# Four edits to the order of high and low weight products and to the PSUM banks of the output mix in a one-core decoder layer

## The chip, the cores and the metric

The kernel runs as one program on one core of a Trainium2 chip. The metric is device time in microseconds, the median of several runs. A core has a matrix engine (TensorE, PE in the rows; its weight loads are PEld), a vector engine (DVE), a scalar engine (ACT), GpSimd (POOL), and a queue engine (SP) that issues most transfers. Each engine runs its own instructions in the order in which the program wrote them and waits for the others by semaphores. Products accumulate in PSUM, of which the program uses eight banks of 128 x 512 fp32 numbers, in two pools of four.

## The reference, cut to what matters

A decoder layer for 256 tokens of width 1024, in fp32, with 256 memory tokens:

```python
z = h @ w_in[l]                      # u (512), q, k, v (512 each)
pool_out = multiscale_pool(u, w_pool[l], pool_scale[l])
attn_out = moba_attention(q, k, v).reshape(B_, S_, ATTN_WIDTH)
mix = jnp.concatenate([pool_out, attn_out], axis=-1) @ w_out[l]
h = layer_norm(DEEPNORM_ALPHA * h + mix, ln1_g[l], ln1_b[l])
h = layer_norm(DEEPNORM_ALPHA * h + memory_cross_attention(h, mem, w_xq[l], w_xkv[l], w_xo[l]), ...)
h = layer_norm(DEEPNORM_ALPHA * h + swiglu(h, w_gate[l], w_up[l], w_down[l]), ...)
```

`u` are the pooling inputs, the first half of `mem @ w_xkv` are the memory keys, `mix` is the output projection of the first block, and the gate and up products of `swiglu` are 11 chunks of 256 + 256 columns.

## The kernel before

**Precision.** Every operand of a product is split in a rounded high part and a remainder, the low part (suffixes h and l in the names): ACT makes the high part (a cast), DVE the low part (a subtraction). A product is high by high, high by low and low by high. `proj_both` takes the token side as one 512-wide moving operand (high and low next to each other), so that a high weight needs one 512-wide matmul (L431) and a low weight one 256-wide matmul (L437).

**Blocks.** The weights of one column chunk come as tiles of several k rows. `proj_both(pss, numbers, yT, group)` does the high matmuls of `group` k rows, two or four matmuls for each, and then the low ones of the same k rows. With group = 8 (KD) all highs of a chunk stand in a row, then all lows. Before the change the pooling inputs (`do_u`, tiles w15 to w18, 2 chunks of two tiles) and the memory keys (`do_xk`, w19 to w26, 4 chunks) use 4, which is one tile of highs, one of lows; the gate and up chunks use 8, the last three of them (w91 to w102) 2, which is one tile as well.

**Weights.** `Stream` fetches raw tiles on SP (7 raw buffers) and prepares them (L184 cast on ACT, L191 subtraction on DVE) into 8 buffers, 9 late in the kernel. It prepares one tile more when a matmul asks for a high row (`get`; every third or second asking in the stages of u and xk) and when a tile is done with (`done`, `next`). So the place of a preparation in the ACT and DVE queues follows from the order in which the matmuls are written.

**Order around the change.** The stages are generators that are run a few steps at a time, with other work written between: `run(u, 4)`, `probs_t(0)`, `run(u, 6)`, `scores(1, 0)` and so on. `scores` puts q k products in two banks (ps), DVE takes them with the maximum (L605), ACT the exponential (L574). `attend` writes po. `split_mem(0)` and `split_mem(4)` split the memory tokens into mT, k rows 0 to 3 and 4 to 7, on ACT (L483) and DVE (L484): the rows print both halves as mT, the order tells them apart as mT_88 and mT_89. The keys of memory use mT: w19, the first tile of a chunk, the first half, w20, the second tile, the second half. `pool_diff` (L657) and `mix_pool` (pm, L661) finish the pooling.

**Banks.** Two pools of four banks each are dealt round robin: `accbank` for the long sums (pu, pxk, acc, xv, m), `bank` for the short ones (ps, pt, po, pm, tp). A tile waits for the last reader of the tile that had its bank before. `project` does the mix (c_mix, w27 to w34) into four accumulators, one for each PIECE (token tile t by column half), first for all four k row by k row, and at the end piece by piece, so that the norm can begin (L768). The last chunk of memory keys holds two accbanks until DVE has taken them (L691, L693).

Of the kernel before, what the change touches and what calls it, by code (L numbers as in the profile page):

```python
# [18 lines left out]
KD = D // P  # L19
# [5 lines left out]
NFC = DFF // CW  # L25
# [25 lines left out]
class Stream:  # L51
# [148 lines left out]
    def get(self, numbers, k):  # L200

        n = self.src[numbers[0]].shape[1]
        self.prepare(numbers[k // n] + 1)
        self.asked += 1
        if not self.held and self.asked % self.pace == 0:
            self.prepare(min(self.used + self.ahead, len(self.tiles) + 1))
        return self.parts_of(numbers, k)
# [18 lines left out]
def decoder_layer(  # L226
# [15 lines left out]
    def a8(name, dt=F32):  # L242
        return ap.tile([P, KD, S], dt, tag="a8", name=name)

    def bank(name):
        return pb.tile([P, 512], F32, tag="b", name=name)

    def accbank(name):
        return pa.tile([P, 512], F32, tag="acc", name=name)
# [4 lines left out]
    def cols(w, c):  # L254

        return ws.add(w[c])

    def rows(w, k0, c0, nk=1, width=D):
        return ws.add(w[k0 * P:(k0 + nk) * P, c0:c0 + width].rearrange("(k p) n -> p k n", p=P), 1)
# [16 lines left out]
    c_u = [cols(w_u, c) for c in range(2)]  # L276
    c_xk = [cols(w_xk, c) for c in range(4)]
    c_mix = [rows(w_out, k, 0) for k in range(KD)]
# [4 lines left out]
    c_xo = [rows(w_xo, k, 0) for k in range(KD)]  # L283
    c_gu = [ws.add(w_gu[c], 4) for c in range(NFC)]
# [38 lines left out]
    xT, mT = Both("xT"), Both("mT")  # L323
# [5 lines left out]
    home = [ap.tile([P, 4, 512], F32, tag="a8", name=f"wr{i}") for i in range(2)]  # L329
# [93 lines left out]
    def proj_both(pss, numbers, yT, group=KD):  # L423

        for k0 in range(0, KD, group):
            for k in range(k0, k0 + group):
                hi, _ = ws.get(numbers, k)
                for b, ps in enumerate(pss):  # L430
                    nc.tensor.matmul(ps, hi[:, b * P:(b + 1) * P], yT.both(k), start=k == 0, stop=False,  # L431
                                     skip_group_check=True)
                yield
            for k in range(k0, k0 + group):
                _, lo = ws.parts_of(numbers, k)
                for b, ps in enumerate(pss):
                    nc.tensor.matmul(ps[:, S:], lo[:, b * P:(b + 1) * P], yT.pair(k)[0], start=False,  # L437
                                     stop=k == KD - 1, skip_group_check=True)
                ws.done(numbers, k)
                if ws.pace == 1:  # L440
                    ws.next()
                yield
# [10 lines left out]
    def proj_rows(acc, chunks, get, pieces, first, last, free, again=False):  # L453

        last_k = sum(ws.rows(numbers) for numbers in chunks) - 1
        k0 = 0
        for numbers in chunks:
            nk = ws.rows(numbers)
            for t in sorted({piece[0] for piece in pieces}):
                for j in range(nk):  # L460
                    k = k0 + j
                    y = pair(get(k), ALL, slice(t * P, (t + 1) * P))
                    hi, lo = ws.get(numbers, j)
                    for piece in pieces:
                        if piece[0] == t:
                            s = slice(*piece[1:])
                            three(acc[piece], y, (hi[:, s], lo[:, s]), first and k == 0, last and k == last_k,
                                  again)
                    if free and t == pieces[-1][0]:
                        ws.done(numbers, j)  # L470
                    yield
            k0 += nk
# [139 lines left out]
    cT = (a8("cTh", F32R), a8("cTl", F32R))  # L612
# [31 lines left out]
    def windows(c):  # L644

        cur, n = upad[:, 2 * c:2 * c + 2, :], 1
        for j, g in enumerate((2 * c, 2 * c + 1)):
            while n < WINDOWS[g]:
                nxt = ep.tile([P, 2, PADW + S], F32, name="win", bufs=4)
                nc.gpsimd.tensor_add(nxt[:, j:, 2 * n - 1:], cur[:, j:, 2 * n - 1:], cur[:, j:, n - 1:PADW + S - n])  # L650
                cur, n = nxt, 2 * n
            sums[g] = cur[:, j, :]
            nc.gpsimd.tensor_mul(sums[g][:, PADW:2 * PADW], sums[g][:, PADW:2 * PADW], fac[:, g, :])
# [20 lines left out]
    def do_u():  # L674
        for c in range(2):
            pss = [accbank("pu") for _ in range(2)]
            yield from proj_both(pss, c_u[c], xT, 4)
            for f, ps in enumerate(pss):
                y = upad[:, 2 * c + f, PADW:]
                nc.scalar.copy(y, ps[:, S:])  # L680
                nc.vector.tensor_add(y, ps[:, :S], y)  # L681
            windows(c)
# [3 lines left out]
    def split_both(hi, lo, left, pss):  # L686

        for f, ps in enumerate(pss):
            nc.scalar.copy(hi[:, f], ps[:, :S])  # L689
        for f, ps in enumerate(pss):  # L690
            nc.vector.tensor_sub(left[:, f], ps[:, :S], r32(hi[:, f]))  # L691
        for f, ps in enumerate(pss):
            nc.vector.tensor_add(lo[:, f], ps[:, S:], left[:, f])  # L693

    def do_xk():
        for c in range(4):
            pss = [accbank("pxk") for _ in range(2)]
            yield from proj_both(pss, c_xk[c], mT, 4)
            left = sp.tile([P, 2, S], F32, name="xkl", tag="pr", bufs=PR_BUFS)
            split_both(*[y[:, 2 * c:2 * c + 2, :] for y in xkT], left, pss)  # L700

# [50 lines left out]
    class Norm:  # L752
# [13 lines left out]
        def sum(self, c0, c1, acc):  # L766
            s = slice(c0, c1)
            nc.vector.scalar_tensor_tensor(self.r[:, s], self.tok[:, s], ALPHA, acc, op0=OP.mult, op1=OP.add)  # L768
# [36 lines left out]
    HALVES = ((0, 512), (512, D))  # L805
    PIECES = tuple((t, *half) for t in range(T) for half in HALVES)

    def project(chunks, get, held, pieces=PIECES):

        acc = {piece: accbank("acc") for piece in PIECES}
        if pieces != PIECES:
            (*_, (_, _, c), _), last = pieces, PIECES[-1]
            acc[pieces[-2]], acc[pieces[-1]] = acc[last][:, :c - last[1]], bank("acc")[:, :last[2] - c]
        head, rest = chunks[:-held], chunks[-held:]
        done = sum(ws.rows(numbers) for numbers in head)
        if head:
            yield from proj_rows(acc, head, get, PIECES, True, pieces != PIECES, True)
        ws.prepare(ws.used + ws.ahead)  # L820
        ws.prepare(ws.used + ws.ahead, nc.gpsimd)
        ws.held = True
        for piece in pieces:
            yield from proj_rows(acc, rest, lambda k: get(done + k), [piece], not head or piece[1] % 512 != 0, True,
                                 piece == pieces[-1], bool(head) and pieces != PIECES)
            yield piece, acc[last] if pieces != PIECES and piece == pieces[-2] else acc[piece]
# [8 lines left out]
    load_norm("g", 1, ln1_g)()  # L835
    load_norm("b", 1, ln1_b)()
    h1 = ap.tile([P, T, D], F32, tag="a8", name="h1")
    mix = project(c_mix, lambda k: (cT[0][:, k], cT[1][:, k]), 4)
    for t in range(T):
        norm = Norm(1, t, xt[:, t, :], h1[:, t, :])  # L840
        for half in HALVES:
# [24 lines left out]
    oT = (a8("oTh", F32R), a8("oTl", F32R))  # L866
# [37 lines left out]
    def xattend(h):  # L904
        po = bank("xo").rearrange("p (d t) -> p d t", d=2)
        for dd in range(2):
            for s in range(2):
                c = h * 256 + dd * P
                three(po[:, dd, :], pair(xv, ALL, s, slice(c, c + P)), pair(xpt[h], ALL, s), s == 0, s == 1)
        split(oT[0][:, 2 * h:2 * h + 2, :], oT[1][:, 2 * h:2 * h + 2, :], po)  # L910
# [17 lines left out]

    h2T = Both("h2T")
    h2 = ap.tile([P, T, D], F32, tag="a8", name="h2")  # L930
    xo = project(c_xo, lambda k: (oT[0][:, k], oT[1][:, k]), 4)
    xattend(1)
    run(xo, 1)
    xprobs_t(2)
# [116 lines left out]
    for c in range(1, NFC):  # L1051
        pss = [(accbank if c % 2 else bank)("pg") for _ in range(4)]
        if c == 3:
            ws.widen(late)
            for i in range(2):
                add_quarters(i)
        gu = proj_both(pss, c_gu[c], h2T, KD if c < NFC - 3 else 2)
        run(gu, 2)
        if left:
            left.multiply()  # L1060
        run(gu, 2)
        if left:
            left.split()
        else:
            run(gu, 4)
            gated_t()
        if c == NFC - 1:
            run(gu, 7)
            ws.held = True
        run(gu)  # L1070
        left = Gated(c, pss)
        left.add()
# [128 lines left out]
    acc = until(dn)  # L1201
# [71 lines left out]
```

## Time and profile before

| | |
|---|---|
| median of 3 runs | 376.22 us (376.06 to 376.52) |
| span of the profiled execution, first to last instruction | 374.4 us |
| left outside the span, median less span | 1.8 us |
| PE busy | 367.9 us, 98% of the span |
| DVE busy | 301.2 us, 80% |
| ACT busy | 206.2 us, 55% |
| chain that ended last | PE 97% |

No time of the profiled execution is given beside its span. A busy PE is a modelled one: a matmul's record is longer than the step to the next, so short waits of PE show as a longer step between two starts rather than as idle time. Times in rows are microseconds from the span's start.

### The profile page before, as it was taken

The numbers are of one execution on the slowest core, as the hardware profiler recorded it, in microseconds if no ns is written. First come the engines' busy times: TensorE is split into PE (matmuls) and PEld (weight loads), VectorE is DVE, ScalarE is ACT, GpSimd is POOL, SyncE is SP. The second block draws the span as 40 slices with busy tenths as digits, with TensorE's granted clock in tenths as the row PEclk, the third lists the DMA queues.
The fourth block names the chain that finished last, engine by engine and source line by source line (L and its number), as shares of the span: only waits on it lengthen the run. The fifth ranks groups of instructions, "written<-read, shape, count | busy, mean of one in ns | idle before, by whom it ended". The sixth has DMA issues, their size and how long they took to land.

```text
span 374.4 us, 5619 instructions
## 1 busy us (share of the span) xinstructions
PE 367.9 (98%) x2058; PEld 317.1 (85%) x2058; DVE 301.2 (80%) x487; ACT 206.2 (55%) x330; POOL 23.6 (6%) x31
## 2 busy tenths in 40 slices
PE   9999999999999999999999999999999999999994
PEld 8997878787888889998888988888888888888882
DVE  6768899975599677875899478888888996999994
ACT  6656677644154645644237456766655575774610
POOL 1000033400020000000112000000000000000012
PEclk9999999999999999999999999999999999999998
DMA  8997684568508964588439999955557463896302
GB/s 279 415 415 268 210 293 136 204 210 285 183 0 271 396 203 141 191 297 306 164 61 293 282 302 335 351 179 175 193 192 251 151 188 98 275 354 258 112 2 112
DMA packets 25819, 84.51 MB, mean 226 GB/s; under 512 B 2624, under 2 KB 3392, under 8 KB 25664
## 3 DMA queue, kind: packets, MB, share of 16 engines
q1 hardware_dynamic: 24528, 78.98, 60.3%
q0 software_dynamic: 832, 4.72, 6.3%
q10 hardware_dynamic: 432, 0.46, 0.4%
q8 instruction: 16, 0.26, 0.3%
q14 instruction: 11, 0.09, 0.1%
HBM read 83.10 MB, written 10.49 MB: 250 GB/s over the span
## 4 chain that ended last, share of the span: by engine, by line
PE 97%; DMA 1%; DVE 1%; ACT 0%; issue 0%; POOLq 0%; ACTq 0%
PE pg L431 20%; PE pg L437 10%; PE pqk L537 6%; PE m L417 5%; PE m L418 5%; PE m L416 5%; PE acc L416 4%; PE acc L417 4%; PE acc L418 4%; PE pxk L431 4%; PE pxq L431 4%; PE pxq L437 2%; PE pu L431 2%; PE pxk L437 2%; PE xv L416 2%; PE xv L418 2%
## 5 line engine op out<-in xcount | busy, mean ns | idle before, releaser
L483 ACT CAST g<-sg 128x512 fp32r<-128x512 f32 x16 | 9.9, 620 | 21.0 <-DVE sg L1037 15.1
L779 POOL TENSOR_TENSOR rs<-rs,mhalf 128x1 f32<-128x1 f32 x6 | 5.0, 833 | 257.6 <-DVE rs L778 257.6
L484 DVE TENSOR_TENSOR g<-sg,g 128x512 fp32r<-128x512 f32 x16 | 11.1, 692 | 9.6 <-ACT g L483 9.6
L1018 DVE TENSOR_TENSOR sg<-pg,sg 128x256 f32<-128x256 f32 x40 | 14.1, 415 | 2.7 <-ACT sg L1017 2.7
L1017 ACT COPY sg<-pg 128x256 f32<-128x256 f32 x40 | 11.8, 376 | 3.8 <-PE pg L437 3.8
L1022 ACT ACTIVATE sg<-sg 128x512 f32<-128x512 f32 x10 | 6.4, 635 | 11.2 <-DVE sg L1018 11.2
L574 ACT ACTIVATE xpr<-xs,mx 128x256 f32<-128x256 f32 x8 | 3.7, 470 | 14.3 <-DVE mx L585 14.3
L574 ACT ACTIVATE pr<-pr,mx 128x128 f32<-128x128 f32 (+1 forms) x16 | 7.1, 445 | 7.6 <-DVE mx L605 7.6
L483 ACT CAST h2T<-tp 128x512 fp32r<-128x512 f32 x4 | 2.3, 587 | 13.0 <-PE tp L494 12.9
L784 DVE SCALAR_TENSOR_TENSOR r<-r,mv,gb 128x512 f32<-128x512 f32 (+2 forms) x12 | 8.2, 722 | 0.0
L771 DVE BATCH_NORM_STATS2 st<-r 128x6 f32<-128x512 f32 (+1 forms) x12 | 8.0, 671 | 0.3
L650 POOL TENSOR_TENSOR win<-upad 128x542 f32<-128x542 f32 x2 | 4.0, 2000 | 57.0 <-DVE upad L681 57.0
L1023 DVE TENSOR_TENSOR sg<-sg 128x512 f32<-128x512 f32 x10 | 6.9, 691 | 0.8
L579 DVE RECIPROCAL sm<-sm 128x2 f32<-128x2 f32 x12 | 2.0, 166 | 6.0 <-ACT xpr L574 4.5
L889 PE MATMUL xs<-xkTh,xq 128*128 128x256 f32 x32 | 6.4, 282 | 0.0
L483 ACT CAST h1T<-tp 128x512 fp32r<-128x512 f32 x4 | 2.4, 588 | 7.2 <-PE tp L494 7.2
L789 DVE SCALAR_TENSOR_TENSOR h<-r,rs,gb 128x512 f32<-128x512 f32 x8 | 5.7, 747 | 0.1
L650 POOL TENSOR_TENSOR win<-win 128x269 f32<-128x269 f32 (+3 forms) x4 | 5.8, 1446 | 0.2
L689 ACT CAST xkTh<-pxk 128x256 fp32r<-128x256 f32 x8 | 2.6, 377 | 5.5 <-PE pxk L437 5.5
L691 DVE TENSOR_TENSOR xkl<-pxk,xkTh 128x256 f32<-128x256 f32 x8 | 3.0, 416 | 3.1 <-ACT xkTh L689 3.1
L889 PEld LDWEIGHTS xs<-xkTh,xq 128*128 128x128 f32 x32 | 5.2, 190 | 0.2
L184 ACT CAST w39h<-w39r 128x1024 fp32r<-128x1024 f32 x1 | 1.0, 1049 | 7.8 <-PE acc L418 7.8
(1137 smaller groups left out, 1289.6 us busy)
## 6 DMA issues: line engine op xcount, KB each, us to landing
sum_z<-in_w_sum SPq DMA_DIRECT2D x2, 1536.0 KB, 9.4
sum_z<-in_w_sum POOLq DMA_DIRECT2D x2, 1536.0 KB, 15.4
gb<-in_ln_g SPq DMA_DIRECT2D x3, 512.0 KB, 7.0
gb<-in_ln_b SPq DMA_DIRECT2D x3, 512.0 KB, 8.3
sum_w<-in_w_sum SPq DMA_DIRECT2D x2, 768.0 KB, 7.5
sum_w<-sum_z POOLq DMA_DIRECT2D x2, 768.0 KB, 9.9
wr<-in_w_qkv SPq DMA_DIRECT2D x5, 256.0 KB, 4.5
mr<-in_mem_t SPq DMA_DIRECT2D x1, 1024.0 KB, 11.7
```

The lines of the kernel that those rows point to most:

```text
L416: nc.tensor.matmul(ps, wa, ya, start=start, stop=False, skip_group_check=part)
L417: nc.tensor.matmul(ps, wa, yb, start=False, stop=False, skip_group_check=part)
L418: nc.tensor.matmul(ps, wb, ya, start=False, stop=stop, skip_group_check=part)
L431: nc.tensor.matmul(ps, hi[:, b * P:(b + 1) * P], yT.both(k), start=k == 0, stop=False, skip_group_check=True)
L437: nc.tensor.matmul(ps[:, S:], lo[:, b * P:(b + 1) * P], yT.pair(k)[0], start=False, stop=k == KD - 1, skip_group_check=True)
L483: nc.scalar.copy(h, ps)
L484: nc.vector.tensor_sub(l, ps, r32(h))
L537: nc.tensor.matmul(qk[i][:, f, :], w[:, c * P:(c + 1) * P], y, start=k == 0 and f == 0 and w is hi and y is x_hi, stop=k == KD - 1 and w i ...
L574: nc.scalar.activation(dst[:, j, :], src[:, j, :], AF.Exp, bias=mx[:, j:j + 1], scale=sign, accum_out=sm[:, j:j + 1])
L889: nc.tensor.matmul(ps[:, t, :], q[:, kk, t * P:(t + 1) * P], k[:, 2 * h + kk], start=n == 0, stop=q is q_lo and kk == 1, skip_group_check= ...
L1017: nc.scalar.copy(y[:, f, :], ps[:, S:])
L1018: nc.vector.tensor_add(y[:, f, :], ps[:, :S], y[:, f, :])
```

## The change

`do_u` and `do_xk` call `proj_both` without a group, so that all eight k rows of highs come first (two tiles of highs, then two of lows). The last three gate and up chunks use 4 in place of 2. `project` takes for each piece the pool of its accumulator: the mix puts the two pieces of token tile 0 in accbanks as before and the two of token tile 1 in banks of the other pool; the second caller, xo, stays with four accbanks.

```diff
-            yield from proj_both(pss, c_u[c], xT, 4)
+            yield from proj_both(pss, c_u[c], xT)
...
-            yield from proj_both(pss, c_xk[c], mT, 4)
+            yield from proj_both(pss, c_xk[c], mT)
...
-    def project(chunks, get, held, pieces=PIECES):
+    def project(chunks, get, held, homes, pieces=PIECES):
...
-        acc = {piece: accbank("acc") for piece in PIECES}
+        acc = {piece: home("acc") for piece, home in zip(PIECES, homes)}
...
-    mix = project(c_mix, lambda k: (cT[0][:, k], cT[1][:, k]), 4)
+    mix = project(c_mix, lambda k: (cT[0][:, k], cT[1][:, k]), 4, (accbank, accbank, bank, bank))
...
-    xo = project(c_xo, lambda k: (oT[0][:, k], oT[1][:, k]), 4)
+    xo = project(c_xo, lambda k: (oT[0][:, k], oT[1][:, k]), 4, (accbank,) * 4)
...
-        gu = proj_both(pss, c_gu[c], h2T, KD if c < NFC - 3 else 2)
+        gu = proj_both(pss, c_gu[c], h2T, KD if c < NFC - 3 else 4)
```

On PE, at the end of the pooling inputs and the beginning of the memory keys (w18 is the last tile of the one, w19 and w20 the first chunk of the other), the order before is:

```order
L437 MATMUL pu<-xT_87,w18l 128x256 x8
L431 MATMUL pxk<-mT_88,w19h 128x512 x8
L437 MATMUL pxk<-mT_88,w19l 128x256 x8
L431 MATMUL pxk<-mT_89,w20h 128x512 x8
L620 MATMUL pt_837<-ident,pr 128x128
L621 MATMUL pt_837<-ident,pr 128x128
L622 MATMUL pt_838<-ident,pr 128x128
```

and with the change:

```order
L437 MATMUL pu<-xT_87,w18l 128x256 x8
L431 MATMUL pxk<-mT_88,w19h 128x512 x8
L431 MATMUL pxk<-mT_89,w20h 128x512 x8
L437 MATMUL pxk<-mT_88,w19l 128x256 x8
L620 MATMUL pt_843<-ident,pr 128x128
L621 MATMUL pt_843<-ident,pr 128x128
L622 MATMUL pt_844<-ident,pr 128x128
```

The first product with the second half of the memory tokens (w20h) stands one block of eight low matmuls earlier.

On ACT, in the second chunk of the pooling inputs, between the two splits of memory tokens, the order before is:

```order
L483 CAST mT_88<-mr 128x4x256
L680 COPY upad<-pu 128x256 x2
L184 CAST w22h<-w22r 128x1024
L574 ACTIVATE pr,sm<-pr,mx 128x256 x4
L483 CAST cTh<-po 128x256
L483 CAST mT_89<-mr 128x4x256
L184 CAST w23h<-w23r 128x1024
L184 CAST w24h<-w24r 128x1024
```

and with the change:

```order
L483 CAST mT_88<-mr 128x4x256
L680 COPY upad<-pu 128x256 x2
L184 CAST w22h<-w22r 128x1024
L184 CAST w23h<-w23r 128x1024
L574 ACTIVATE pr,sm<-pr,mx 128x256 x4
L483 CAST cTh<-po 128x256
L483 CAST mT_89<-mr 128x4x256
L184 CAST w24h<-w24r 128x1024
```

The cast of w23 has moved ahead of the exponentials, and so ahead of the second half of the memory tokens.

DVE, which makes the low parts, has the same place. Before (L605 reads the scores):

```order
L484 TENSOR_TENSOR mT_88<-mr,mT_88 128x4x256
L681 TENSOR_TENSOR upad<-pu,upad 128x256 x2
L191 TENSOR_TENSOR w22l<-w22r,w22h 128x1024
L605 ISA pr,mx<-ps_722,tri 128x256
L605 ISA mx 128x1
```

and with the change:

```order
L484 TENSOR_TENSOR mT_88<-mr,mT_88 128x4x256
L681 TENSOR_TENSOR upad<-pu,upad 128x256 x2
L191 TENSOR_TENSOR w22l<-w22r,w22h 128x1024
L191 TENSOR_TENSOR w23l<-w23r,w23h 128x1024
L605 ISA pr,mx<-ps_728,tri 128x256
L605 ISA mx 128x1
```

The subtraction of w23 has moved ahead of the reading of the scores; the rows from there to the low part of mT_89 are the same in both, and w23l stood right behind L657, which follows mT_89, before. Further moves of the same kind: w21 goes ahead of the scores before these, w26 and w28 ahead of two copies of transposed probabilities, w31 and w33 behind the evacuation of memory keys, and of the last gate chunks w100, w104 and w108 behind the split of the gated chunk. On SP the two loads of the first norm's gains go ahead of the fetch of w40. POOL has the same order.

## Rows read from the trace of the kernel before

**Rows 1.** The page: busy time by engine, and the chain that ended last by engine.

```profile
PE 367.9 (98%) x2058; PEld 317.1 (85%) x2058; DVE 301.2 (80%) x487; ACT 206.2 (55%) x330; POOL 23.6 (6%) x31
...
PE 97%; DMA 1%; DVE 1%; ACT 0%; issue 0%; POOLq 0%; ACTq 0%
```

**Rows 2.** Timeline, mix's beginning: start, us, engine, line, operation, tiles [idle before <-releaser].

```profile
85.45 0.39 PE L418 MATMUL acc<-w27h,cTl 128*128 128x512 f32 x1
...
86.01 0.47 PE L416 MATMUL acc<-w27h,cTh 128*128 128x512 f32 x1 [0.17 <-DVE xkTl L693]
...
86.31 0.40 PE L417 MATMUL acc<-w27l,cTh 128*128 128x512 f32 x1
...
86.55 0.39 PE L418 MATMUL acc<-w27h,cTl 128*128 128x512 f32 x1
```

**Rows 3.** Windows: stretch, us, busy by engine; three gate chunks of each group.

```profile
223.45:256.79 33.34, 33.34 (x194) 29.53 (x193) 27.69 (x46) 20.93 (x34) 0.84 (x1) 1.00 0.83 288
279.02:312.54 33.52, 33.52 (x193) 29.50 (x193) 28.32 (x44) 20.21 (x35) 0.00 (x0) 1.00 0.59 179
```

**Rows 4.** Timeline of PE, first chunk of the memory keys.

```profile
56.81 2.00 PE L431 MATMUL pxk<-mT,w19h 128*128 128x512 f32 x8
58.66 1.12 PE L437 MATMUL pxk<-mT,w19l 128*128 128x256 f32 x8
59.61 2.01 PE L431 MATMUL pxk<-mT,w20h 128*128 128x512 f32 x8
```

**Rows 5.** Timeline of DVE ahead of and behind the second split of memory tokens.

```profile
52.35 1.22 DVE L191 TENSOR_TENSOR w22l<-w22r,w22h 128x1024 fp32r<-128x1024 f32 x1
53.48 0.42 DVE L605 CUSTOM_DVE_ANT_0 pr<-ps,tri 128x256 f32<-128x256 f32 x1
...
57.33 1.22 DVE L484 TENSOR_TENSOR mT<-mr,mT 128x1024 fp32r<-128x1024 f32 x1
...
59.14 1.22 DVE L191 TENSOR_TENSOR w23l<-w23r,w23h 128x1024 fp32r<-128x1024 f32 x1
```

**Rows 6.** Timeline of ACT in the same stretch.

```profile
50.94 1.07 ACT L184 CAST w22h<-w22r 128x1024 fp32r<-128x1024 f32 x1
54.01 0.51 ACT L574 ACTIVATE pr<-pr,mx 128x256 f32<-128x256 f32 x1 [2.00 <-DVE mx L605]
```

**Rows 7.** The tile w23r: its issue (start 39.0 us) and its landing.

```profile
L114 SPq DMA_DIRECT2D w23r<-in_w_xk x1: 328/328/328, 39.0 to 39.0; - x1
...
DMA to landing us min/median/max: 3.9/3.9/3.9
```

**Rows 8.** Timeline, DVE and PE: two pooling products (pm) and what stands around them.

```profile
69.14 0.94 DVE L657 SCALAR_TENSOR_TENSOR upad<-win,upad 128x256 f32<-128x256 f32 x1 [0.27 <-POOL win L653]
...
69.80 0.40 PE L638 MATMUL po<-sb,vt 128*64 128x128 f32 x4
70.23 0.67 PE L661 MATMUL pm<-upad,pool_w 128*128 128x256 f32 x2
70.55 1.30 PE L437 MATMUL pxk<-mT,w22l 128*128 128x256 f32 x8
...
74.10 0.39 PE L638 MATMUL po<-sb,vt 128*64 128x128 f32 x4
...
74.77 1.30 PE L437 MATMUL pxk<-mT,w23l 128*128 128x256 f32 x8
```

**Rows 9.** Timeline of DVE and PE from the last gate chunks on.

```profile
285.68 1.23 DVE L191 TENSOR_TENSOR w100l<-w100r,w100h 128x1024 fp32r<-128x1024 f32 x1 [0.18 <-ACT w100h L184]
...
290.08 1.23 DVE L191 TENSOR_TENSOR w101l<-w101r,w101h 128x1024 fp32r<-128x1024 f32 x1 [0.25 <-PE pg L437]
...
312.68 1.42 DVE L1018 TENSOR_TENSOR sg<-pg,sg 128x256 f32<-128x256 f32 x4 [2.70 <-ACT sg L1017]
...
345.41 1.22 DVE L157 TENSOR_TENSOR w128l<-w129r,w128h 128x1024 fp32r<-128x1024 f32 x1
...
347.99 0.39 PE L417 MATMUL m<-w128l,g 128*128 128x512 f32 x1
```

## The prediction, written before the result was known

> **What bounds the kernel now.** I read the page first: PE is busy 98% of the span and makes 97% of the chain that ended last [rows 1]. So the time is the sum of PE's steps, and an edit counts only where it changes a step of PE. ACT and DVE matter where they hand PE something late. I then read, for each edit, how long PE's steps are at its place (timelines and windows), and for every operand that is now wanted earlier, or made later, how much cover it has (timelines of DVE and ACT beside that of PE).
>
> **Part 1, banks of the mix.** The mix's seventh matmul opens the first accumulator of token tile 1. It starts 0.56 us behind the sixth (85.45 to 86.01), where later ones follow each other by 0.24; the row names DVE's xkTl, the evacuation of the last memory keys, as what it waited for. The step after the restart is 0.30, again above 0.24 [rows 2]. The steady step is nearer 0.23, so the two steps hold 0.56 + 0.30 - 2 x 0.23 = 0.40 us too much. In the other pool the next two banks last held po and pm of the third chunk, products that stand before 70.55 [rows 8] and are read soon after, over 10 us ahead, so the wait goes and nothing takes its place: **-0.40 us**. Between 0 (another wait at the same spot) and -0.40 I take the whole, since the row names one releaser. The pool is next needed by the transposes of h1, behind the norm which reads these very sums: no cost. The sums of xv, next in accbanks, get two banks that are free earlier.
>
> **Part 2, a switch from low to high weights.** Three gate chunks with all highs in a row take 33.34 us, the last three, of the same 192 matmuls, 33.52 [rows 3]. These have four blocks of highs each, so nine more returns from low to high: 0.18 / 9 = 0.02 us each. With group 4 the last three keep two blocks each, 6 returns fewer: **-0.12 us**. In the pooling inputs and memory keys the change takes away at most six returns, one per chunk. But in five of the six a score, a transpose, po or pm stands between the blocks, or the wait of part 3, and restarts the row of highs anyway; only w25 and w26 follow each other clean. I take **-0.02 us**, between 0 and -0.12, nearest to the one clean pair.
>
> The Trainium skill, page "TensorE: Matmul & The Clock Gate", section "Wait — 56ns, not 53.3ns?", speaks against this part: a warm matmul costs its columns at 2.4 GHz plus a fixed 2.5 ns or so, whatever stood before it, so that no order of the same matmuls is worth more than another. By it parts 1 to 4 would sum to +0.76 us instead of +0.62. The two windows, which differ by 0.18 us over the same matmuls, speak for the row.
>
> **Part 3, an operand that is wanted earlier and made later.** w20h is the first matmul that reads the second half of the memory tokens (mT_89, high and low). Before, the block w19l covers it: w20h starts at 59.61 [rows 4], and DVE ends the low half at 57.33 + 1.22 = 58.55 [rows 5], 1.06 us earlier. The change moves both ends.
>
> PE's end: w20h now follows w19h at once, at 58.66, where w19l stood [rows 4]. What PE does ahead of it is reordered within the pooling inputs, the same matmuls with as many restarts, so I leave that time as it is.
>
> DVE's end: w23l is put ahead of the scores' reading. In the run of DVE from there to mT the chain is tight: w22l at 52.35, L605 at 53.48, then softmax, po's low part, mT at 57.33, with no wait except short ones for ACT inside the softmax, which come again. A subtraction takes 1.13 us of DVE's queue, as the step from w22l's start to L605's shows (52.35 to 53.48); w23l is the same operation with the same 1.22 [rows 5]. So L605 starts at 54.61 and the low half of mT ends at 58.55 + 1.13 = 59.68. Its high half on ACT comes behind the exponentials and moves with them. The cast w23h fits into ACT's 2.00 us of idle time ahead of L574 [rows 6], at about 52, and its raw tile is there (issued at 39.0, landed 3.9 later [rows 7]); so ACT adds nothing to the 1.13. What holds this chain at its beginning is the first po on PE, not DVE, so moving w21l ahead elsewhere doesn't bring it forward.
>
> From DVE's end to PE's start I take 0.15 us, the step from L657's end (69.14 + 0.94 = 70.08) to pm's start at 70.23 [rows 8]. PE can start w20h at 59.68 + 0.15 = 59.83, and wants to at 58.66: a wait of 1.17 us, and 0.07 for the restart as in part 1 (0.30 against 0.23): **+1.24 us**. The lows of w19, which could have filled it, are written behind w20h. Lower bound: were w23l free, 58.55 + 0.15 - 58.66 = 0.04 us. Upper bound: were its cast in line with the exponentials too, another 0.95 us (50.94 to the next cast, a cast of 1.07 less overlap [rows 6]), 2.2 us. I take 1.24, since DVE's queue is full and ACT's is not.
>
> **Part 4, what the later PE meets.** In the third chunk of keys, pm waits for DVE's L657, which waits for POOL. From po's second half to the next lows takes 0.75 us there (69.80 to 70.55), and 0.67 in the fourth chunk (74.10 to 74.77) [rows 8]. POOL's sums begin behind an evacuation that DVE does at the same time as before (w23l is only moved from behind mT to ahead of it). With PE over 1 us later this wait ends: **-0.08 us**. DVE does w26l and w28l ahead of it now, which puts L657 at about 70.0, and PE comes at about 71.5.
>
> **Part 5, at no cost.** w100, w104 and w108 are prepared behind the split of a gated chunk, some 3.3 us later (before, the split filled DVE from 285.68 + 1.13 to 290.08). w100 belongs to the last gate chunk, which begins over 10 us after that, and DVE stands idle 2.70 us when the last gate sums arrive [rows 9], so it catches up. Two gains' loads on SP ahead of w40's fetch: the norm behind the mix wants the gains, and w40 belongs to the stage after the mix, so neither is near its use. The tightest cover of the end is w128l, ready at 345.41 + 1.22 = 346.63 and wanted at 347.99, 1.36 us [rows 9]; DVE's work there begins with PE's last gate sums and moves with PE, so this is kept.
>
> **The sum.** -0.40 - 0.12 - 0.02 + 1.24 - 0.08 = +0.62 us. All of it lies on PE, so the profiled span goes from 374.4 to 375.0. The median lies 1.8 us above the span, outside of what changes: 376.22 + 0.62 = **376.84 us**, 0.16% slower. About 0.2% of this kernel, 0.75 us, is what a measurement can tell from no change; the forecast lies inside.
>
> **The rivals.**
>
> *A, the cover holds.* If w23l costs the chain nothing, because DVE or ACT has a gap there that I don't see, the wait shrinks to the lower bound of 0.04: -0.40 - 0.12 - 0.02 + 0.04 = -0.50, **375.72 us**. For it: every other preparation moved has many microseconds of cover. Against it: DVE's rows follow each other without idle time. Here the change does what its words say, and no more.
>
> *B, DVE comes late at the end.* The split of two gated chunks now stands ahead of w100 and w104, about 3.3 us each. If these delays are carried on rather than made up, 6.6 us reach the stage of the down weights, less DVE's idle 2.70 and the cover of 1.36 at w128l [rows 9]: PE waits 2.5 us, **379.3 us**, slower by 0.8%. It decides from 4.1 us of carried delay on. Against it: the DVE has the same work in that stage, only in another order, and the order is the same again from w109 on.
>
> *C, the row of highs is worth nothing.* Then part 2 falls and the sum is +0.76, **376.98 us**, just over 0.2% slower. For it, the rule that I weighed above; against it, the windows [rows 3].
>
> **Chances.** Forecast 0.75, A 0.13, B 0.04, C 0.08. The forecast's own uncertainty is the wait, some 0.3 us either way, and 0.15 for the medians. About a quarter of it lies beyond 376.97, none below 375.47; of A a third lies below. Slower by over 0.2%: 0.19 + 0.04 + 0.04 = 0.27. Faster by over 0.2%: 0.05. Within: 0.68. The range from 376.1 to 377.4 holds the forecast with its spread and C; it leaves out A and B, and is short of the upper bound of part 3.
>
> **What would show it.** In the profile after, the chain should name DVE's mT ahead of w20h, near 59 us, with a step of PE of about 1.2 us more; L605 of the scores should start near 54.6; the step of 0.56 at the mix should be 0.23; each of the last three gate chunks should take 11.13 us instead of 11.17; pm of the third chunk should wait for nothing. Wrong would be: no long step at w20h (A), a step over 1.5 us there (ACT in line), or steps of PE over 0.3 us in the down weights (B).

## The result, and the profile after

The changed kernel takes 378.69 us (378.03 to 379.22, median of 5 runs) beside 376.41 (376.06 to 376.66, 5 runs) of the kernel before on the same chip: a ratio of 1.0056 [1.0044, 1.0067], 0.56% slower, +1.7 to +2.5 us. The profiled spans are 376.3 and 374.4 us, 1.9 us apart, where the medians are 2.28 apart: the profiled execution of after, with 378.13 us, is one of its quicker ones. What follows explains the 1.9; the rest lies in executions without a trace. The forecast was 376.84 us, 0.62 us above the 376.22 us it started from, with a range up to 377.4, 1.2 us above; the time lies outside. The sign was the one that I forecast, the size was more than three times as large.

PE is busy for the same 367.9 us as before [rows 1], but its part of the chain that ended last falls from 97% to 95%:

```profile
PE 95%; DVE 1%; ACT 1%; DMA 1%; issue 1%; POOLq 0%; SPq 0%; ACTq 0%
```

What PE waited for, after (engine, tile, line <- releaser: us in total, times, longest):

```profile
PE pxk L431 <- DVE mT L484: 1.7, 1, 1.7
...
PE pm L661 <- ACT cTh L483: 0.6, 1, 0.6
```

The wait of the mix for xkTl [rows 2] is gone. Two are new: the first memory keys wait for mT, as forecast, and a pooling product (pm) waits, which was not forecast. PE's timeline of after, from the first memory keys to the third chunk, and below it the row of before that ends the first stretch:

```profile
56.80 2.00 PE L431 MATMUL pxk<-mT,w19h 128*128 128x512 f32 x8
60.55 2.11 PE L431 MATMUL pxk<-mT,w20h 128*128 128x512 f32 x8 [1.75 <-DVE mT L484]
62.50 1.11 PE L437 MATMUL pxk<-mT,w19l 128*128 128x256 f32 x8
63.45 0.27 PE L620 MATMUL pt<-ident,pr 128*128 128x128 f32 x1
...
71.80 0.40 PE L638 MATMUL po<-sb,vt 128*64 128x128 f32 x4
72.75 0.67 PE L661 MATMUL pm<-upad,pool_w 128*128 128x256 f32 x2 [0.56 <-ACT cTh L483]
73.08 1.30 PE L437 MATMUL pxk<-mT,w22l 128*128 128x256 f32 x8
```

```profile
61.45 0.27 PE L620 MATMUL pt<-ident,pr 128*128 128x128 f32 x1
```

From w19h to the first transpose it takes 63.45 - 56.80 = 6.65 us; before, 61.45 - 56.81 = 4.64 [rows 4]. That is +2.01 for the same 24 matmuls. PE wanted w20h 1.85 us behind w19h, at 58.65, and got it at 60.55: a wait of 1.90. From there to po's second half (L638) both kernels take 8.35 us (61.45 to 69.80 in [rows 8], here 63.45 to 71.80). Then po's second half to the low matmuls of w22 takes 1.28 us (71.80 to 73.08) against 0.75 [rows 8]: +0.53. From these lows to the sixth matmul of the mix both take 14.90 us (70.55 to 85.45 in [rows 8] and [rows 2], here 73.08 to 87.98). The sixth, seventh and ninth matmul of the mix, after:

```profile
87.98 0.39 PE L418 MATMUL acc<-w27h,cTl 128*128 128x512 f32 x1
88.20 0.39 PE L416 MATMUL acc<-w27h,cTh 128*128 128x512 f32 x1
...
88.66 0.39 PE L418 MATMUL acc<-w27h,cTl 128*128 128x512 f32 x1
```

Sixth to ninth is 0.68 us; before it was 1.10 (85.45 to 86.55 [rows 2]): -0.42. Last, the chain of after where the three chunks of gates begin and end (start, us, what):

```profile
281.11 3.65 PE pg L431 x16
...
314.50 0.23 PE m L416
```

They take 314.50 - 281.11 = 33.39 us, against 33.52 [rows 3]: -0.13.

| term | forecast | in the traces |
|---|---|---|
| banks of the mix | -0.40 | -0.42 |
| switches, last three gate chunks | -0.12 | -0.13 |
| switches, u and keys | -0.02 | 0.00 |
| w20h waits for mT, with the restart | +1.24 | +2.01 |
| pm of the third chunk | -0.08 | +0.53 |
| sum | +0.62 | +1.99 |

The sum is, within 0.1 us, the 1.9 us between the spans. Two terms are off, both wait for DVE, and both have one origin. DVE of after (first fence), and POOL of after (second) and of before (third), in the same stretch:

```profile
52.33 1.21 DVE L191 TENSOR_TENSOR w22l<-w22r,w22h 128x1024 fp32r<-128x1024 f32 x1
53.46 2.11 DVE L191 TENSOR_TENSOR w23l<-w23r,w23h 128x1024 fp32r<-128x1024 f32 x1
55.49 0.41 DVE L605 CUSTOM_DVE_ANT_0 pr<-ps,tri 128x256 f32<-128x256 f32 x1
...
59.26 1.23 DVE L484 TENSOR_TENSOR mT<-mr,mT 128x1024 fp32r<-128x1024 f32 x1
...
64.01 2.11 DVE L191 TENSOR_TENSOR w26l<-w26r,w26h 128x1024 fp32r<-128x1024 f32 x1
...
69.51 1.77 DVE L191 TENSOR_TENSOR w28l<-w28r,w28h 128x1024 fp32r<-128x1024 f32 x1
...
72.20 0.41 DVE L657 SCALAR_TENSOR_TENSOR upad<-win,upad 128x256 f32<-128x256 f32 x1
```

```profile
52.49 1.99 POOL L650 TENSOR_TENSOR win<-upad 128x542 f32<-128x542 f32 x1 [50.46 <-DVE upad L681]
54.57 1.09 POOL L653 TENSOR_TENSOR win<-win,fac 128x16 f32<-128x16 f32 x1
```

```profile
52.52 2.00 POOL L650 TENSOR_TENSOR win<-upad 128x542 f32<-128x542 f32 x1 [50.48 <-DVE upad L681]
54.59 0.22 POOL L653 TENSOR_TENSOR win<-win,fac 128x16 f32<-128x16 f32 x1
```

w23l takes 2.11 us where every subtraction of [rows 5] takes 1.22. It begins at 53.46 and ends at 55.57; POOL's addition ends at 54.48, and 55.57 - 54.48 = 1.09 is about one subtraction, by the step of 1.13 from w22l to w23l. POOL's L653, on 16 columns, took 0.22 before and takes 1.09 now, up to 55.66, just behind the end of w23l. Before, L605 stood in w23l's place (53.48 [rows 5]), beside the same POOL addition, and took its usual 0.42; L605 reads PSUM, the subtraction two operands in SBUF. The reading is that the two kinds of instruction exclude each other, a whole instruction at a time, and that a row's duration holds its wait: here w22l, POOL's addition, w23l and L653 went one after the other. (POOL's addition holds a wait too: 1.99 us beside w22l, where a like one on 538 columns, beside operations that read PSUM, took 1.08 at 64.32 in before.) w26l (2.11) and w28l (1.77) meet POOL's next sums in the same way, and L657, behind them, comes at 72.20 instead of the 70.0 that I reckoned with. It ends at 72.61, and pm starts at 72.75: L657 is what pm waited for, not the ACT copy that the row names, for that one reads po and writes cTh, which pm doesn't read; in two runs below the same wait names L657.

The two engines don't always alternate. POOL and DVE of before, at the place of w26l and w27l:

```profile
65.48 3.33 POOL L650 TENSOR_TENSOR win<-win 128x530 f32<-128x530 f32 x1
```

```profile
65.52 1.22 DVE L191 TENSOR_TENSOR w26l<-w26r,w26h 128x1024 fp32r<-128x1024 f32 x1
66.65 1.22 DVE L191 TENSOR_TENSOR w27l<-w27r,w27h 128x1024 fp32r<-128x1024 f32 x1
```

Both subtractions keep their 1.22, and POOL's addition, which takes 1.07 in after (at 67.14), takes 3.33: it waited for two subtractions in a row (1.07 + 2 x 1.13 = 3.33). The three runs below that have this order of DVE show the same 3.33. So in before POOL paid for the meeting with w26l, where PE doesn't notice, and in after w26l paid. What decides who goes first no run here settles. L657, which reads two tiles in SBUF as well, shows the price too: in before it takes 0.94 [rows 8] beside POOL's next addition, which ends at 69.80, and less than half of that in the fourth chunk, without POOL:

```profile
71.89 0.41 DVE L657 SCALAR_TENSOR_TENSOR upad<-win,upad 128x256 f32<-128x256 f32 x1
```

### The profile page after: what moved, and what is told of

Read it like the earlier page. It is cut to its first block, busy times and chain, and to the rows that moved or that the text cites. A ratio compares the mean times of both kernels' runs of the same rounds, so it can differ in the third digit from the quotient of the medians.

```text
span 376.3 us, 5613 instructions
## 1 busy us (share of the span) xinstructions
PE 367.9 (98%) x2058; PEld 317.6 (84%) x2058; DVE 303.0 (81%) x487; ACT 206.5 (55%) x330; POOL 24.8 (7%) x31
## 4 chain that ended last, share of the span: by engine, by line
PE 95%; DVE 1%; ACT 1%; DMA 1%; issue 1%; POOLq 0%; SPq 0%; ACTq 0%
PE pg L431 19%; PE pg L437 10%; PE pqk L537 6%; PE m L416 5%; PE m L417 5%; PE m L418 5%; PE acc L416 4%; PE acc L417 4%; PE acc L418 4%; PE pxq L431 4%; PE pxk L431 3%; PE pxk L437 2%; PE pxq L437 2%; PE xv L416 2%; PE xv L418 2%; PE xv L417 2%
## 5 line engine op out<-in xcount | busy, mean ns | idle before, releaser
L650 POOL TENSOR_TENSOR win<-upad 128x542 f32<-128x542 f32 x2 | 4.0, 1998 | 57.0 <-DVE upad L681 57.0
L691 DVE TENSOR_TENSOR xkl<-pxk,xkTh 128x256 f32<-128x256 f32 x8 | 3.0, 416 | 4.5 <-ACT xkTh L689 4.5
L650 POOL TENSOR_TENSOR win<-win 128x269 f32<-128x269 f32 (+3 forms) x4 | 5.4, 1344 | 0.2
```

## The experiments

Single profiles differ by up to 0.8 us ahead of anything that is edited here (the first products of the pooling inputs, w15h, begin at 40.50 in before, at 41.30 in one of the runs below). So I compare stages in the traces, not spans: **A** is from w19h to the first transpose behind it (4.64 us before, 6.65 after), **S** from w19h to the first matmul of w28 in the mix. S is 87.46 - 56.81 = 30.65 us before and 89.56 - 56.80 = 32.76 after. Times are medians, of this run and of the kernel before on the same chip. Each ratio is the recorded estimate with its 95% interval; it can differ by up to 0.001 from the quotient of the two medians.

**POOL's window sums left out.** The changed kernel without L650 and L653; its window sums are missing.

```diff
-                nxt = ep.tile([P, 2, PADW + S], F32, name="win", bufs=4)
-                nc.gpsimd.tensor_add(nxt[:, j:, 2 * n - 1:], cur[:, j:, 2 * n - 1:], cur[:, j:, n - 1:PADW + S - n])
-                cur, n = nxt, 2 * n
+                n = 2 * n
...
-            nc.gpsimd.tensor_mul(sums[g][:, PADW:2 * PADW], sums[g][:, PADW:2 * PADW], fac[:, g, :])
```

> The changed kernel without the window sums of the pooling on POOL (additions at L650 and the products with the edge factors at L653 are left out, so the pooled part of the output is not the layer's); all other instructions are kept. Theory 1 (the subtraction w23l waits for POOL's additions in its new place, since both want the same access to SBUF): w23l takes 1.22 us instead of 2.11, the scores' L605 starts at 54.6 instead of 55.5, PE's step at w20h has 1.2 us too much instead of 1.9, pm of the third chunk of keys doesn't wait, and the time is the predicted one, 0.5 to 0.6 us above before. Rival (w23l is long for a reason of its own in that place: its cast, its raw tile, its buffer): w23l stays at 2.1 us and the time at 1.5 us above before or more.

377.17 us against 376.34, ratio 1.0021 [1.0012, 1.003]. DVE, then PE:

```profile
53.92 1.22 DVE L191 TENSOR_TENSOR w23l<-w23r,w23h 128x1024 fp32r<-128x1024 f32 x1
```

```profile
57.26 2.00 PE L431 MATMUL pxk<-mT,w19h 128*128 128x512 f32 x8
60.12 2.12 PE L431 MATMUL pxk<-mT,w20h 128*128 128x512 f32 x8 [0.86 <-DVE mT L484]
...
71.38 0.40 PE L638 MATMUL po<-sb,vt 128*64 128x128 f32 x4
72.05 1.30 PE L437 MATMUL pxk<-mT,w22l 128*128 128x256 f32 x8
```

w23l is back at 1.22 and takes 1.14 us of the queue (L605 starts at 55.06), w20h is 1.01 late (60.12 against 57.26 + 1.85), and po to the lows is 0.67: nothing waits at pm (L657 has no sums to wait for here). A is 5.76, +1.12. The median, +0.83 us, is near my forecast of +0.62. S is 31.27, +0.62, and with the -0.12 of the gates (33.40 us) the change would cost +0.50. So the forecast holds within 0.2 us for a kernel in which POOL does nothing there; what it missed is POOL.

**POOL's first sum cut in two.** Taking POOL away could help in other ways than by ending this wait. If DVE waits for the end of one POOL instruction, a POOL instruction of half the columns must shorten w23l though POOL's work is the same.

```diff
-                nc.gpsimd.tensor_add(nxt[:, j:, 2 * n - 1:], cur[:, j:, 2 * n - 1:], cur[:, j:, n - 1:PADW + S - n])
+                for a, b in ((2 * n - 1, 136), (136, PADW + S)) if n == 1 else ((2 * n - 1, PADW + S),): nc.gpsimd.tensor_add(nxt[:, j:, a:b], cur[:, j:, a:b], cur[:, j:, a - n:b - n])
```

> The changed kernel with the first window addition on POOL cut into two instructions of half the columns each (same result). Theory 1 (w23l waits until POOL's addition in hand is done, so the wait is as long as that addition): w23l takes about 1.6 us instead of 2.1, L605 starts 0.5 us earlier against w22l, PE's step at w20h has 1.4 us too much instead of 1.9. Rival (meeting POOL costs a fixed 0.9 us, whatever the length of POOL's instruction): w23l stays at 2.1 us.

377.19 us against 376.44, ratio 1.0029 [1.0017, 1.0041]. DVE, POOL, PE:

```profile
54.19 1.66 DVE L191 TENSOR_TENSOR w23l<-w23r,w23h 128x1024 fp32r<-128x1024 f32 x1
```

```profile
53.22 3.12 POOL L650 TENSOR_TENSOR win<-upad 128x270 f32<-128x270 f32 x2 [51.19 <-DVE upad L681]
```

```profile
57.52 2.00 PE L431 MATMUL pxk<-mT,w19h 128*128 128x512 f32 x8
60.82 2.14 PE L431 MATMUL pxk<-mT,w20h 128*128 128x512 f32 x8 [1.29 <-DVE mT L484]
```

w23l takes 1.66, between 1.22 and 2.11, and w20h is 60.82 - 59.37 = 1.45 late, against 1.90 and 1.01. The two halves take POOL 3.12 us, longer than the whole sum's 1.99, since w23l now stands between them. That is what the reading gives: each waits until the other's instruction is done, and a shorter instruction of POOL means a shorter wait of DVE. A fixed price of 0.9 us for a meeting, the rival, would have left w23l at 2.11. S is 31.75, 1.01 less than in after: 0.45 of it at w20h, most of the rest at pm, which hardly waits here (po's second half to the lows 0.73).

**The two halves of the row of highs, each alone.** First the pooling inputs alone, with the keys, the gates and the banks as before:

```diff
-            yield from proj_both(pss, c_u[c], xT, 4)
+            yield from proj_both(pss, c_u[c], xT)
```

> Only the pooling inputs with eight rows of highs, memory keys, gates and banks as before. So w23l stands ahead of the scores, but w19l still stands ahead of w20h. Theory 1 (operand late, by its queue and by POOL): w23l takes 2.1 us, mT's second half ends near 60.5, w20h wants to start at 59.6, so PE waits 1.0 us and 0.08 for the restart: about 1.1 us slower than before. Rival (w23l's place costs PE nothing by itself, only the moved w20h does): no step at w20h, the time of before within 0.1 us.

377.27 us against 376.34, ratio 1.0024 [1.0015, 1.0034]. w23l takes 2.11 us on DVE. PE:

```profile
59.35 1.11 PE L437 MATMUL pxk<-mT,w19l 128*128 128x256 f32 x8
61.26 2.11 PE L431 MATMUL pxk<-mT,w20h 128*128 128x512 f32 x8 [0.80 <-DVE mT L484]
```

w23l is moved by this half, and it alone uses up the cover: w20h, behind w19l as before, starts 1.91 behind it instead of 0.95, a wait of 0.96. A is 5.70 (+1.06), S 31.63 (+0.98): with PE later and w26l and w28l in their old places, po's second half to the lows takes 0.67 instead of 0.75. Then the keys alone:

```diff
-            yield from proj_both(pss, c_xk[c], mT, 4)
+            yield from proj_both(pss, c_xk[c], mT)
```

> Only the memory keys with eight rows of highs, pooling inputs, gates and banks as before. So w20h comes 0.95 us earlier, but w23l stands behind mT as before; w26l and w28l stand ahead of L657 of the third pooling group. Theory 1 (these meet POOL's additions and each other): next to no wait at w20h (below 0.1 us); w26l takes about 2.1 us, L657 ends near 71.8, and pm of the third chunk, which PE reaches near 70.2, waits 1.5 to 1.8 us; 1.5 to 1.8 us slower than before. Rival (no lock, only the queue): L657 ends near 70.4, pm waits 0.3 us, 0.3 us slower than before.

378.23 us against 376.34, ratio 1.0049 [1.0031, 1.0066]. PE and DVE:

```profile
58.61 2.05 PE L431 MATMUL pxk<-mT,w20h 128*128 128x512 f32 x8
...
71.90 0.67 PE L661 MATMUL pm<-upad,pool_w 128*128 128x256 f32 x2 [1.67 <-DVE upad L657]
```

```profile
63.16 2.11 DVE L191 TENSOR_TENSOR w26l<-w26r,w26h 128x1024 fp32r<-128x1024 f32 x1
...
68.67 1.77 DVE L191 TENSOR_TENSOR w28l<-w28r,w28h 128x1024 fp32r<-128x1024 f32 x1
...
71.35 0.41 DVE L657 SCALAR_TENSOR_TENSOR upad<-win,upad 128x256 f32<-128x256 f32 x1
```

Here w20h comes straight behind w19h and doesn't wait (A 4.69), though it is wanted 0.95 earlier: mT comes in time as long as w23l stands behind it. But w26l and w28l stand ahead of L657 and are long, and pm waits 1.67 us; here the row names L657 itself. S is 32.35 (+1.70). The two halves and the banks, 0.98 + 1.70 - 0.42 = 2.26, make the 2.11 of after within 0.15. In after PE is already late from w20h when it comes to pm, which covers a part of that wait: po's second half to the lows grows by 0.53 instead of 1.64.

**The parts that gain.** The banks alone (only the edits of `project` and of its two callers):

```diff
-        acc = {piece: accbank("acc") for piece in PIECES}
+        acc = {piece: home("acc") for piece, home in zip(PIECES, homes)}
...
+    mix = project(c_mix, lambda k: (cT[0][:, k], cT[1][:, k]), 4, (accbank, accbank, bank, bank))
```

> The banks alone: the kernel before with two mix accumulators in the other pool, all groups as before. Theory 1 (the term of the prediction holds): the step of 0.56 us at the mix's seventh matmul becomes 0.23, nothing takes its place, 0.40 us faster than before, span 374.0. Rival: the wait comes back at the next place where the pools meet (the first transposes of h1 or the sums of xv), then the time is that of before, within 0.1 us.

376.10 us against 376.34, ratio 0.9992 [0.9983, 1.0001]. The trace shows it more sharply than the median. PE:

```profile
57.23 2.00 PE L431 MATMUL pxk<-mT,w19h 128*128 128x512 f32 x8
...
85.87 0.39 PE L418 MATMUL acc<-w27h,cTl 128*128 128x512 f32 x1
86.10 0.39 PE L416 MATMUL acc<-w27h,cTh 128*128 128x512 f32 x1
...
87.46 0.39 PE L416 MATMUL acc<-w28h,cTh 128*128 128x512 f32 x1
```

The step is 0.23 instead of 0.56, and S is 30.23, -0.42. Then the banks with the last gates, u and the keys as before:

```diff
-        gu = proj_both(pss, c_gu[c], h2T, KD if c < NFC - 3 else 2)
+        gu = proj_both(pss, c_gu[c], h2T, KD if c < NFC - 3 else 4)
```

> Banks of the mix and the last three gate chunks, pooling inputs and memory keys as before. Theory 1 (terms of the prediction hold): -0.40 and -0.12 us, 0.5 us faster than before, no new wait anywhere. Rival (the moved preparations of w100, w104, w108 come late in the down stage): steps of PE over 0.3 us there and a time at or above before.

376.26 us against 376.44, ratio 0.9991 [0.9981, 1.0001]; S is 30.22 and the gates take 33.40 us (278.98 to 312.38), so the trace holds 0.43 + 0.12 = 0.55 us of gain, of which this median shows 0.18. Whether the two are faster at all this run doesn't settle, since the interval reaches 1.0001.

**The cover restored.** If the order of DVE is the cause, the change must cost nothing once preparations are held back there. `held` stops the preparation of further tiles; here from the middle of the second pooling chunk until mT is written:

```diff
-    run(u, 6)
+    run(u, 3); ws.held = True; run(u, 3)
...
-    split_mem(4)
+    split_mem(4); ws.held = False
```

> The changed kernel, all four parts, but the preparation of weights is held from the middle of the second pooling chunk until the second half of mT is split. So w23l and the tiles behind it go back to the places that they had before, behind mT and behind L657 of the third group. Theory 1 (the loss comes from the preparations that the longer rows of highs drew ahead, not from the order of the matmuls): no wait above 0.1 us at w20h, none at pm; banks, gates and w25/w26 keep their gain: 0.4 to 0.6 us faster than before. Rival (the rows of highs themselves leave PE without cover): a step of 1 us or more remains at w20h or pm and the time is that of before or above.

376.29 us against 376.44, ratio 1.0001 [0.9992, 1.0009]. PE and DVE:

```profile
58.67 2.04 PE L431 MATMUL pxk<-mT,w20h 128*128 128x512 f32 x8
...
70.82 0.67 PE L661 MATMUL pm<-upad,pool_w 128*128 128x256 f32 x2 [0.57 <-DVE upad L657]
```

```profile
70.26 0.41 DVE L657 SCALAR_TENSOR_TENSOR upad<-win,upad 128x256 f32<-128x256 f32 x1
```

The first wait is gone (w20h 1.84 behind w19h at 56.83), the second stays: L657 ends at 70.67, and pm is wanted 0.43 behind po's second half [rows 8], at 69.85 + 0.43 = 70.28. S is 30.79. The loss against before is gone, the gain is not there: what I expected came half true. The subtractions meet POOL here too, only others of them (w25l takes 2.11, w27l 1.75, both ahead of L657). L657 is also written behind `probs_t(3)` and `mix_pool(1)`, whose copies (L625, L663) stand ahead of it on DVE, so I moved it ahead of them as well, and ran beside it the kernel of banks and gates once more:

```diff
+    pool_diff(2)
     probs_t(3)
     mix_pool(1)
-    pool_diff(2)
```

> The version with the held preparation, and the third group's L657 written ahead of the transposed probabilities and the pooling product of the second group, where POOL's sum for it is done (66.6 us in the held version). Theory 1: the 0.57 us wait at pm ends too, all other gains stay: 0.6 us faster than before in the trace, ratio near 0.998. Rival: L657 now waits for POOL, or holds up the copy behind it, and the wait only moves: time of before within 0.1 us.

> Banks and gates again, beside the version above on the same chip. Theory 1: -0.40 and -0.12 us, 0.5 us faster than before, ratio near 0.9987. Rival: no difference from before, within 0.1 us.

On this chip before has 376.82. All parts with the cover restored: 375.70, ratio 0.9973 [0.9963, 0.9983]. Banks and gates alone: 375.61, ratio 0.9972 [0.9960, 0.9984]. Both beat the kernel before; the changed kernel, not run on this chip, had lost to it with 1.0056. PE of the kernel with the cover restored, and below it of banks and gates alone:

```profile
57.63 2.00 PE L431 MATMUL pxk<-mT,w19h 128*128 128x512 f32 x8
59.47 2.06 PE L431 MATMUL pxk<-mT,w20h 128*128 128x512 f32 x8
...
70.67 0.40 PE L638 MATMUL po<-sb,vt 128*64 128x128 f32 x4
71.34 1.30 PE L437 MATMUL pxk<-mT,w22l 128*128 128x256 f32 x8
```

```profile
70.31 0.39 PE L638 MATMUL po<-sb,vt 128*64 128x128 f32 x4
71.08 1.30 PE L437 MATMUL pxk<-mT,w22l 128*128 128x256 f32 x8
```

No wait at w20h (1.84 behind w19h), none at pm (0.67, where the other has 0.77). S is 30.19, and 30.24 in the other. These 0.05 us are not the worth of the rows of highs: the step at pm is 0.10 shorter, where L657 was moved, and A is 0.04 longer (4.68 against 4.64). In u, from w15h to w19h, both take 16.33. So the rows of highs in u and the keys gain nothing that these traces show, even where they cost no wait. The same kernel of banks and gates gave 0.9991 on one chip and 0.9972 on another, with intervals that barely overlap; the trace's 0.55 us, 0.15%, lies in the first and just above the second's upper end of 0.9984.

## Why the prediction was wrong, point by point

- **Bound.** Right: PE's steps add up to the time, and the five terms, read from PE alone, give the spans' difference within 0.1 us.
- **Part 1, banks.** Right in place and size: -0.42 in after, -0.42 alone.
- **Part 2, switches.** Right for the last gates: -0.13. By the rule of the Trainium skill that I weighed against it (page "TensorE: Matmul & The Clock Gate", section "Wait — 56ns, not 53.3ns?") the same matmuls would have taken as long in either order; the windows of 33.52, 33.39 and 33.40 us disagree. In u and the keys there was nothing to win: the run with the cover restored shows no gain there beside banks and gates alone.
- **Part 3, w20h.** The mechanism and the place were right: the chain names mT ahead of w20h, and the trace with only w23l moved waits there. The term that was mis-sized is "A subtraction takes 1.13 us of DVE's queue". I read that from w22l, which began just ahead of POOL's sums and didn't wait for them. In its new place w23l took 2.03 us of the queue (53.46 to 55.49), and L605 began at 55.49, not at 54.6. With 1.17 + 0.90 the wait would have been 2.07; it was 1.90, since the chain behind it was 0.08 shorter (L605 to mT 3.77 us, before 3.85) and the hand-off 0.06 (60.49 to 60.55) instead of 0.15. That my upper bound of 2.2 us held the size was luck: I put it on a cast of ACT in line, and ACT had no part. L605 started the moment that w23l ended.
- **Part 4, pm.** Wrong in sign: I wrote that L657 would come "at about 70.0" behind w26l and w28l at 1.13 each. They took 2.11 and 1.77, and the queue was 0.8 late already (w25l at 62.88 instead of 62.07): 0.9 + 0.55 + 0.8 is the 2.2 us from 70.0 to 72.20. The end of the small wait that I forecast is real: with the pooling inputs alone the step is 0.67. The trace before had shown the price: L657 itself took 0.94 there [rows 8], more than twice its 0.41 in the fourth chunk. I used that row for a hand-off and didn't ask why it was so long.
- **Part 5.** Right, nothing waits for w100 to w108 or for the gains.
- **Rivals.** Rival A didn't happen; the last run with the cover restored comes to its size (S and gates 0.46 + 0.12 us shorter than before), but by taking w23l out of the way and not by a gap. B didn't happen: no new wait behind the mix. Rival C fell with the gates' -0.13, though in u and the keys it came true.
- **The range.** It left out the upper bound of part 3 on purpose. Had I carried the 2.2 us into it, it would have ended at 377.8 and would still have missed: the second wait, at pm, was not among the cases. What I should have asked of a subtraction put in a new place is what POOL does at that time.

## What to carry to other kernels

Cost an instruction by its rows at the place it moves to, not at the place it comes from: look which other engine works there. A row that is longer than its like (0.94 for 0.41) is a price to be explained before anything is moved near it. And where a preparation is moved ahead, look at who stands behind it on its engine; here a gain on PE forecast at 0.02 us, and not found, was paid with waits of 1.9 and 0.5 us for DVE.

## What the runs showed of the hardware

DVE's subtractions and sums of two SBUF operands and POOL's sums exclude each other, a whole instruction at a time, and the wait stands inside the duration of the one that waits, not as idle time ahead of it: 2.11 us for 1.22 on DVE, 1.66 with POOL's instruction halved, 1.22 without POOL; on POOL 1.09 us for 0.22, and 3.33 for 1.07 behind two subtractions in a row. So they don't strictly alternate, and which engine pays differs from place to place. Operations of DVE with an operand in PSUM keep their time beside POOL's sums: L605 its 0.42 us, and L691, a subtraction of an SBUF from a PSUM operand, 0.41 (at 67.04 in after), with POOL's sum at its 1.07.

The Trainium skill, page "SBUF — State Buffer", section "Who interferes with whom", says that a DVE instruction with two SBUF inputs contends with a GpSimd instruction that reads SBUF for a shared port pair, and that the pair is an exclusive lock for the whole instruction. These runs agree with the exclusion, with the numbers just given; it would have told me to look at POOL, and I didn't weigh it. That the ports are the cause, rather than something else that makes the two take turns, no run here shows by itself.
